# Moving the forget gate's chain from the pa projection into the v projection, and the norm's token-half sums to pa's second block

## The chip, the cores and the metric

The kernel runs on one core of one Trainium2 chip. The metric is the device time of one execution in microseconds, the median of several runs. Five engines work side by side, each in the order of its own instruction queue: TensorE (PE, matmuls), VectorE (DVE), ScalarE (ACT), GpSimd (POOL) and SyncE (SP), which here only issues DMAs. SBUF is the on-chip working memory, PSUM holds matmul results in eight banks.

## The reference

One layer of a hybrid encoder on x of 512 tokens by 1024 channels, in float32. What the change touches is the first part:

```python
h = rms_norm(x, mix_norm_pre[layer])
proj = jnp.einsum("bsd,de->bse", h, w_in[layer])
xa, ga, q, k, v, f_logit, g_a, g_b = jnp.split(proj, offs, axis=-1)
...
y_a = jax.nn.gelu(ga) * hr
y_b = forgetting_attention(q, k, v, f_logit + b_forget[layer])
merged = (jax.nn.sigmoid(g_a + b_merge[layer, 0]) * jnp.einsum("bse,ed->bsd", y_a, w_proj_a[layer])
          + jax.nn.sigmoid(g_b + b_merge[layer, 1]) * jnp.einsum("bse,ed->bsd", y_b, w_proj_b[layer]))
...
cum = jnp.cumsum(jax.nn.log_sigmoid(f_logit.astype(jnp.float32)), axis=1).transpose(0, 2, 1)
sc = sc + cum[:, :, qs:qe, None] - cum[:, :, None, :qe]
```

Here hr is the RG-LRU's scan over the convolved xa, 1280 channels wide. The forget gate is a projection of h onto 16 columns, one for each head, then log-sigmoid and a running sum over the tokens. Its result is needed as an additive bias when the attention scores are made, far behind the projections.

## The kernel before, in words

The normalised h is kept transposed in SBUF as two parts, hh (rounded to float32r) and hl (the rest), each 128 partitions by 8 by 512. A weight tile likewise becomes wh and wl: DMA into raw, ACT rounds it to wh (L198), DVE subtracts to get wl (L201). A product is three matmuls, wh·hh, wh·hl and wl·hh (mm3, L243).

The list `order` (L212) fixes the sequence of weight tiles: xa (10 tiles), v (8 units), ga (10), pa (16 units of 640 columns), q and k. `unit(name)` (L237) gives a tile and fetches two ahead; raw, wh and wl have four buffers each, so a tile's split waits for matmuls on the one four before it. `background` (L173) lets POOL make a small copy from a weight tile and issue one or two transfers for the last stage.

Outside blocks under `manual_schedule`, the framework's planner fixes every engine's order before the run: an instruction that comes earlier in the program goes first as soon as its inputs are there by the planner's own estimates. On the chip each engine then keeps that order and waits on semaphores. Pools with `reuse_waits="tile"` hand over memory tile by tile: a new tile waits for the last users of the tiles that lay there before. Pools on side "right" are stacked from the other end of SBUF.

The stages around the change, in the order of the program:

- Line 741: xa, with the RG-LRU's convolution (pool xc), its gate matmuls (`gate_mm`, three tiles behind, pool rgw), and at the end the first half of v, with the last gates between its units.
- Line 804: `v_out(0)` empties v's first four banks; then the second half of v in four units (L806), with tanh and exp of the RG-LRU on ACT (`batch`, in an order held together by `last_act`) and `inflow` on DVE.
- Line 816: ga, ten tiles; beside them sqrt, the scans (DVE, L789 and L790) and `gate_out` (gelu on ACT, product and split on DVE), which gives yh and yl. Pools rtanh (ten tiles tt) and gelu are on the right, in the scope rg2.
- Line 903: pa, y_a @ w_proj_a, in 16 steps of `PA_ORDER`: half 0 of columns 0 to 2, half 1 of columns 0 to 2, then alternating. Behind the matmuls of each step `early_sums(step)` is called.
- Line 956: q0 and k0, then the gates gA and gB by a seven-product scheme in a hand-written order, which needs sums of h's quarters.

Before the change, `early_sums(3)` called `forget()` (L832) and closed rg2. `forget` loads the 16 columns (L837), splits them into a 48-column tile fw (POOL memset L839, ACT L840, DVE L841), makes 16 matmuls (L844, L845), and runs a chain of small operations on 16 partitions by 512: ACT copy, bias add, log1p of exp by a series (L296 to L310, with one reciprocal and one Exp), a scan over the tokens (L856), and a reordering into keys (L858), which four DMAs on SP write to DRAM (L860). Its tiles came from rtanh's slots (tag "tt"). At step 3 the pools gkeep, gsum and hf were opened, in memory that rtanh and gelu had. The quarter sums of hh + hl, tiles hf (L883, L885 and two steps of `sub`, L351), were formed at steps 6 to 11, the first gate pair was loaded at 12 and its weight sums formed at 13.

Of the kernel before, what the change touches and what calls it, by code (L numbers as in the profile page):

```python
# [8 lines left out]
F32 = mybir.dt.float32  # L9
F32R = mybir.dt.float32r  # L10
BF16 = mybir.dt.bfloat16
AF = mybir.ActivationFunctionType
ALU = mybir.AluOpType
# [3 lines left out]
P = 128  # L17
S = 512
D = 1024
KD = D // P  # L20
NT = S // P
# [5 lines left out]
H = 16  # L27
# [8 lines left out]
C_CFW, C_CFB, C_MA, C_MB, C_BF = 80, 224, 272, 280, 288  # L36
# [17 lines left out]
PO = [0, 128, 384, 768, 1280]  # L54
# [7 lines left out]
def turns(ap, d=HT):  # L62

    if ap.shape[-1] == 2 * d:
        return ap.rearrange("p (a i) -> p i a", a=2)
    return ap.rearrange("p (t a i) -> p t i a", a=2, i=d)


def parted(ap, d=HT):

    if ap.shape[-1] == 2 * d:
        return ap.rearrange("p (i a) -> p a i", a=2)
    return ap.rearrange("p (t i a) -> p t a i", a=2, i=d)


def placed(ap, d=HT):

    if ap.shape[-1] == 2 * d:
        return ap.rearrange("p (a i) -> p a i", a=2)
    return ap.rearrange("p (t a i) -> p t a i", a=2, i=d)  # L80
# [7 lines left out]
def kernel(  # L88
# [15 lines left out]
    nc = tc.nc  # L104
    act, dve, pool, pe = nc.scalar, nc.vector, nc.gpsimd, nc.tensor
# [17 lines left out]
    def bank(name):  # L123
        return pspools[-1].tile([P, 512], F32, tag="ps", name=name)
# [12 lines left out]
    cpt = cpool.tile([P, NC], F32, name="cpt")  # L137
# [99 lines left out]
    def unit(name, ahead=2):  # L237

        i = where[name]
        fetch(i + ahead)  # L240
        return ready.pop(name)
# [54 lines left out]
    def log1p_exp_neg(z, tl):  # L296
        y = tl("y")
        dve.scalar_tensor_tensor(out=y, in0=z, scalar=-1.0, in1=z, op0=ALU.mult, op1=ALU.max)
        act.activation(out=y, in_=y, func=AF.Exp, scale=-1.0)
        d = tl("d")  # L300
        dve.tensor_scalar(out=d, in0=y, scalar1=2.0, scalar2=None, op0=ALU.add)
        dve.reciprocal(d, d)
        s = tl("s")
        dve.tensor_tensor(out=s, in0=y, in1=d, op=ALU.mult)
        dve.tensor_tensor(out=d, in0=s, in1=s, op=ALU.mult)
        dve.tensor_scalar(out=y, in0=d, scalar1=1.0 / 17.0, scalar2=None, op0=ALU.mult)
        for c in (15, 13, 11, 9, 7, 5, 3):
            dve.scalar_tensor_tensor(out=y, in0=y, scalar=1.0 / c, in1=d, op0=ALU.add, op1=ALU.mult)
        dve.scalar_tensor_tensor(out=s, in0=y, scalar=1.0, in1=s, op0=ALU.add, op1=ALU.mult)
        return s  # L310
# [5 lines left out]
    hh = hpool.tile([P, KD, S], F32R, name="hh")  # L316
    hl = hpool.tile([P, KD, S], F32R, name="hl")
# [6 lines left out]
    def v_start(c):  # L324
        for p in range(4 * c, 4 * c + 4):
            vt[p] = vpools[c].tile([P, NT, 4, HD], F32R, tag="vy", name=f"v{p}")
        return [bank(f"v{c}_{t}") for t in range(NT)]

    def v_mm(u, pv, w):
        wh, wl = w  # L330
        for t in range(NT):
            tok = slice(t * P, (t + 1) * P)
            for i in range(2):
                k = 2 * u + i
                pe.matmul(pv[t], hh[:, k, tok], turns(wh[:, i], SH), start=k == 0, stop=False)  # L335
                pe.matmul(pv[t], hh[:, k, tok], turns(wl[:, i], SH), start=False, stop=False)  # L336
                pe.matmul(pv[t], hl[:, k, tok], turns(wh[:, i], SH), start=False, stop=k == KD - 1)

    def v_out(c, pv):
        for t in range(NT):  # L340
            pvv = pv[t].rearrange("p (q j d) -> p q j d", q=4, j=2)
            for q in range(4):
                p = 4 * c + q
                vh = vt[p][:, t, 0:4:3, :]
                act.copy(vh, pvv[:, q])
                dve.tensor_tensor(out=vt[p][:, t, 1:3, :], in0=pvv[:, q], in1=vh.bitcast(F32), op=ALU.subtract)
# [3 lines left out]
    def sub(out, a, b):  # L350
        dve.tensor_tensor(out=out, in0=a, in1=b, op=ALU.subtract)  # L351
# [173 lines left out]
    with ExitStack() as rg:  # L525
        rt, ixt, tt = {}, {}, {}
# [267 lines left out]
        def gate_out(t):  # L794
# [6 lines left out]
            dve.tensor_tensor(out=placed(yl[t], SH), in0=parted(gl, SH), in1=placed(yh[t].bitcast(F32), SH),  # L801
                              op=ALU.subtract)

        v_out(0, pv)
        pv = v_start(1)
        for u in range(4):  # L806
            w = unit(f"v1_{u}")
            v_mm(u, pv, w)
            background(1, w)
            for t in range(5 * u // 2, 5 * (u + 1) // 2):  # L810
                batch([rg_tanh(t), rg_exp(t)])
                inflow(t)
        v_out(1, pv)
        steps = {0: (range(0, 4), ()), 1: (range(4, TR), range(0, 2)), 2: ((), range(2, 5)), 3: ((), range(5, 7)), 4: ((), range(7, 9)), 5: ((), range(9, TR))}
        outs = {2: (0,), 3: (1,), 4: (2, 3), 5: (4,), 6: (5,), 7: (6, 7), 8: (8,), 9: (9,)}
        for t in range(TR):
# [10 lines left out]

        papool = mstk.enter_context(tc.tile_pool(name="pa", bufs=1, reuse_waits="tile"))
        pa = papool.tile([P, KD, S], F32, name="pa")
        cnd = ctx.enter_context(tc.tile_pool(name="cnd", bufs=1, space=bass.MemoryType.DRAM)).tile([H, PO[NT]], F32, name="cnd")  # L830

        def forget():  # L832
            def tl(name, n=H, dt=F32):
                return tpool.tile([P, S], dt, tag="tt", name=f"f_{name}")[0:n]

            fr = tl("fr", P)[:, : KD * H].rearrange("p (k e) -> p k e", k=KD)
            nc.sync.dma_start(fr, w_f)  # L837
            fw = tl("fw", P, F32R)[:, : KD * 48].rearrange("p (k e) -> p k e", k=KD)
            pool.memset(fw[:, :, H:32].bitcast(F32), 0.0)  # L839
            act.copy(fw[:, :, 0:H], fr)  # L840
            dve.tensor_tensor(out=fw[:, :, 32:48], in0=fr, in1=fw[:, :, 0:H].bitcast(F32), op=ALU.subtract)  # L841
            pf = bank("f")
            for k in range(KD):
                pe.matmul(pf[0:48], fw[:, k], turns(hh[:, k]), start=k == 0, stop=False)  # L844
                pe.matmul(pf[0:48], fw[:, k], turns(hl[:, k]), start=False, stop=k == KD - 1)  # L845
            z = tl("z")
            act.copy(z, pf[32:48])
            dve.scalar_tensor_tensor(out=z, in0=pf[0:H], scalar=cpt[0:H, C_BF : C_BF + 1], in1=z, op0=ALU.add, op1=ALU.add)
            with tc.issue_after(last_act[0].ins):
                l1p = log1p_exp_neg(z, tl)  # L850
            dve.tensor_scalar(out=z, in0=z, scalar1=0.0, scalar2=None, op0=ALU.min)
            dve.scalar_tensor_tensor(out=z, in0=l1p, scalar=-2.0, in1=z, op0=ALU.mult, op1=ALU.add)
            ones = tl("ones")
            pool.memset(ones, 1.0)
            cum = tl("cum")
            dve.tensor_tensor_scan(out=cum, data0=ones, data1=z, initial=0.0, op0=ALU.mult, op1=ALU.add)  # L856
            keys = tl("keys")
            dve.tensor_scalar(out=placed(keys), in0=parted(cum), scalar1=-8.0, scalar2=None, op0=ALU.mult)  # L858
            for b in range(NT):
                nc.sync.dma_start(cnd[:, PO[b] : PO[b + 1]], keys[:, : PO[b + 1] - PO[b]])  # L860

        tgpool = mstk.enter_context(tc.tile_pool(name="tg", bufs=3, reuse_waits="tile"))
        gdram = ctx.enter_context(tc.tile_pool(name="gdram", bufs=1, space=bass.MemoryType.DRAM))
# [3 lines left out]
        gp = {}  # L867
# [2 lines left out]
        fq = []  # L870

        def early_sums(step):
            if step == 3:
                forget()
                rg2.close()
                gates.kpool = dstk.enter_context(tc.tile_pool(name="gkeep", bufs=2, reuse_waits="tile"))
                gates.tpool = sumstk.enter_context(tc.tile_pool(name="gsum", bufs=2, reuse_waits="tile"))
                hfpool = hfstk.enter_context(tc.tile_pool(name="hf", bufs=1, reuse_waits="tile"))
                fq.extend(hfpool.tile([P, KH, SH], F32, name=f"hf{i}") for i in range(4))
            elif 6 <= step < 10:  # L880
                i = step - 6
                k, c = (slice(0, KH), slice(KH, KD))[i % 2], (X, Y)[i // 2]
                dve.tensor_tensor(out=fq[i], in0=hh[:, k, c].bitcast(F32), in1=hl[:, k, c].bitcast(F32), op=ALU.add)  # L883
            elif step == 10:
                dve.tensor_tensor(out=fq[3], in0=fq[2], in1=fq[3], op=ALU.add)  # L885
                sub(fq[2], fq[0], fq[2])
            elif step == 11:
                sub(fq[0], fq[3], fq[0])
                sub(fq[1], fq[1], fq[0])
            elif step == 12:  # L890
                gp[0] = Pair(gates, 0, GP[0])
            elif step == 13:
                gp[0].sums(0)
                gp[0].sums(1)
            elif step == 14:
                gp[0].sums_hi(0)
                gp[0].sums_lo(0)
            elif step == 15:
                gp[0].sums_hi(1)
                gp[0].sums_lo(1)  # L900
# [896 lines left out]
```

## Time and profile before

| what | before |
|---|---|
| median of 3 runs | 887.05 us (886.27 to 887.78) |
| the profiled execution | 886.33 us, of it span 884.6 us |
| PE busy in the span | 871.0 us, 98% |
| DVE busy | 744.6 us, 84% |
| ACT busy | 611.1 us, 69% |
| v, second half on PE | 106.8 to 127.5 us |
| ga on PE | 127.5 to 179.3 us |
| pa with f's matmuls on PE | 179.3 to 234.6 us |
| granted PE clock in these stages | 1.00 |

A line of the timeline has the start in the span, the duration, the engine, the source line, the operation and the tiles as out<-in; a bracket at its end gives the engine's idle time before it and what ended that. A matmul's duration is modelled and overlaps the next one: a matmul of 512 columns starts 0.216 us after the one before it.

### The profile page before, as it was taken

What the parts mean: (1) busy time and instruction counts of PE and PEld (TensorE: products, weight loads), DVE (VectorE), ACT (ScalarE), POOL (GpSimd) and SP (SyncE); (2) the same over time, 40 slices, a digit from 0 to 9 for tenths busy, and PEclk for the clock granted to TensorE, in tenths of its full rate; (3) what the DMA queues carried; (4) which work ended last, traced back from release to release, by engine and by line L of the source; (5) the groups of instructions that cost most, each with busy time, mean ns of one, the idle gap of its engine ahead of it and who ended that gap; (6) DMA issues with size and microseconds to landing.
All of it is one profiled execution on the core that took longest, in us unless ns stands there. A gap on an engine that the chain in (4) does not pass through costs nothing.

```text
span 884.6 us, 15833 instructions
## 1 busy us (share of the span) xinstructions
PE 871.0 (98%) x5856; PEld 794.5 (90%) x5856; DVE 744.6 (84%) x1209; ACT 611.1 (69%) x1031; POOL 215.4 (24%) x278
## 2 busy tenths in 40 slices
PE   9999999999999999999999999999999999999996
PEld 7888888888899988888888889999999999988885
DVE  7986469738978849998868699999999999889997
ACT  6575595533466648776755497888888888688774
POOL 3344334536011013121104100233332332100000
PEclk9999999999999999999999999999999999999999
DMA  7787689999874377353506663778898898699864
GB/s 268 231 273 220 172 228 258 238 277 197 192 182 135 116 261 274 132 171 129 202 26 202 218 200 107 175 183 236 217 222 244 211 226 208 223 399 307 276 192 149
DMA packets 71040, 185.24 MB, mean 209 GB/s; under 512 B 7153, under 2 KB 27681, under 8 KB 70578
## 3 DMA queue, kind: packets, MB, share of 16 engines
q1 hardware_dynamic: 47360, 127.72, 43.2%
q0 software_dynamic: 23456, 56.37, 29.3%
q8 instruction: 46, 0.75, 0.3%
q14 instruction: 32, 0.26, 0.1%
q10 hardware_dynamic: 146, 0.14, 0.0%
HBM read 150.69 MB, written 35.73 MB: 211 GB/s over the span
## 4 chain that ended last, share of the span: by engine, by line
PE 85%; DVE 9%; ACT 2%; issue 2%; DMA 1%; DVEq 0%; SPq 0%; ACTq 0%
PE up L458 7%; PE up L456 7%; PE up L455 7%; PE dn L1500 2%; PE dn L1499 2%; PE dn L1498 2%; PE ga L245 2%; PE ga L244 2%; PE ga L246 2%; DVE al L351 2%; PE pa L245 2%; PE pa L244 2%; PE v L335 2%; PE v L336 2%; PE xa L244 2%
## 5 line engine op out<-in xcount | busy, mean ns | idle before, releaser
L1370 DVE SCALAR_TENSOR_TENSOR u<-up,cpt,u 128x511 f32<-128x511 f32 x96 | 71.3, 745 | 3.5 <-ACT u L1364 1.8
L391 POOL DMA_DIRECT2D ml<-raw_up x42 | 36.2, 861 | 148.1 <-ACT ml L390 88.8
L1500 PE MATMUL dn<-wh_dn,al 128*128 128x512 f32 (+1 forms) x180 | 66.5, 369 | 1.2 <-DVE al L351 1.2
L1499 PE MATMUL dn<-wl_dn,ah 128*128 128x512 f32 (+1 forms) x180 | 66.2, 368 | 0.5 <-DVE wl_dn L201 0.4
L1498 PE MATMUL dn<-wh_dn,ah 128*128 128x512 f32 (+1 forms) x180 | 65.7, 365 | 0.0
L455 PE MATMUL up<-sh,th 128*128 128x256 f32 x252 | 59.5, 275 | 0.0
L456 PE MATMUL up<-sl,th 128*128 128x256 f32 x252 | 59.5, 275 | 0.0
L201 DVE TENSOR_TENSOR wl_dn<-raw_dn,wh_dn 128x1024 fp32r<-128x1024 f32 x42 | 51.1, 1217 | 5.0 <-ACT wh_dn L198 5.0
L351 DVE TENSOR_TENSOR tl<-t,th 128x1024 fp32r<-128x1024 f32 x42 | 51.1, 1218 | 0.0
L1364 ACT ACTIVATE u<-up,cpt 128x512 f32<-128x512 f32 x48 | 36.9, 778 | 19.9 <-PE up L458 10.0
L455 PEld LDWEIGHTS up<-sh,th 128*128 128x128 f32 x252 | 48.4, 192 | 0.0
L456 PEld LDWEIGHTS up<-sl,th 128*128 128x128 f32 x252 | 48.4, 192 | 0.0
L198 ACT CAST wh_dn<-raw_dn 128x1024 fp32r<-128x1024 f32 x42 | 44.3, 1054 | 4.7 <-DMA raw_dn<-td 2.8
L437 ACT CAST th<-t 128x1024 fp32r<-128x1024 f32 x42 | 43.8, 1045 | 2.6 <-DVE t L351 0.6
L1378 POOL TENSOR_TENSOR yf<-u,u 128x512 f32<-128x512 f32 x23 | 30.4, 1323 | 58.8 <-issue 46.0
L1500 PEld LDWEIGHTS dn<-wh_dn,al 128*128 128x128 f32 x180 | 34.1, 189 | 7.5 <-DVE al L351 3.5
L456 PE MATMUL up<-h2l,mh 128*128 128x256 f32 x168 | 39.7, 275 | 0.0
L455 PE MATMUL up<-h2h,mh 128*128 128x256 f32 x168 | 39.7, 275 | 0.0
L1499 PEld LDWEIGHTS dn<-wl_dn,ah 128*128 128x128 f32 x180 | 34.1, 189 | 6.0 <-DVE wl_dn L201 1.8
L1054 ACT ACTIVATE P<-P,mx 128x384 f32<-128x384 f32 (+3 forms) x64 | 35.2, 552 | 5.1 <-DVE mx L1049 5.1
L458 PE MATMUL up<-sh,tl 128*128 128x256 f32 x252 | 38.4, 275 | 0.0
L1498 PEld LDWEIGHTS dn<-wh_dn,ah 128*128 128x128 f32 x180 | 34.1, 189 | 4.0
(729 smaller groups left out, 3230.2 us busy)
## 6 DMA issues: line engine op xcount, KB each, us to landing
raw_up<-in_w_up_dram SPq DMA_DIRECT2D x48, 512.0 KB, 5.3
td<-in_w_down_dram POOLq DMA_DIRECT2D x36, 512.0 KB, 7.1
raw_dn<-td SPq DMA_DIRECT2D x24, 512.0 KB, 4.9
ml<-raw_up POOLq DMA_DIRECT2D x21, 512.0 KB, 5.3
B<-cnd POOLq DMA_DIRECT2D x16, 640.0 KB, 5.4
raw_dn<-in_w_down_dram SPq DMA_DIRECT2D x18, 512.0 KB, 4.2
raw_wo<-in_w_out_dram SPq DMA_DIRECT2D x16, 512.0 KB, 4.2
td<-td POOLq DMA_DIRECT2D x12, 512.0 KB, 12.5
```

The costliest lines, as they stand in the source:

```text
L198: act.copy(self.wh, self.raw)
L201: engine.tensor_tensor(out=self.wl, in0=self.raw, in1=self.wh.bitcast(F32), op=ALU.subtract)
L244: pe.matmul(dst, ah, bh, start=first, stop=False)
L351: dve.tensor_tensor(out=out, in0=a, in1=b, op=ALU.subtract)
L437: act.copy(self.th[i], self.t[i])
L455: pe.matmul(dst, wh[:, k], turns(ah[:, k]), start=first and k == 0, stop=False, skip_group_check=True)
L456: pe.matmul(dst, wh[:, k], turns(al[:, k]), start=False, stop=False, skip_group_check=True)
L458: pe.matmul(dst, wl[:, k], turns(ah[:, k]), start=False, stop=k == KH - 1, skip_group_check=True)
L1370: dve.scalar_tensor_tensor(out=c[:, s:], in0=ps[:, : S - s], scalar=col(C_CFW + 3 * e + j), in1=c[:, s:], op0=ALU.mult, op1=ALU.add)
L1498: pe.matmul(d[:, x], ah[:, k, tok], bh, start=first, stop=False, skip_group_check=True)
L1499: pe.matmul(d[:, x], ah[:, k, tok], bl, start=False, stop=False, skip_group_check=True)
L1500: pe.matmul(d[:, x], al[:, k, tok], bh, start=False, stop=last, skip_group_check=True)
```

## The change

`forget()` becomes a generator with two stops: the first part loads and splits the weights, makes the matmuls and takes the tile z; the second adds the bias and runs the log1p series; the third does the rest and writes the keys. It is advanced at the head of the last v units 0, 1 and 2, ahead of that unit's matmuls in the program. Its tiles come from a pool of their own, "forget", one buffer for each of nine names (2 KB a partition each), opened on the right side when v's second half starts and closed behind `v_out(1)`.

In pa, rg2 is closed and the three pools are opened at step 0; the quarter sums stand at steps 1 to 6 (before 6 to 11), the first gate pair's load at step 11 (before 12) and its weight sums at step 12 (before 13). The splits at 14 and 15 stay.

```diff
+        cnd = ctx.enter_context(tc.tile_pool(name="cnd", bufs=1, space=bass.MemoryType.DRAM)).tile([H, PO[NT]], F32, name="cnd")
+        def forget():
+            def tl(name, n=H, dt=F32):
+                return fpool.tile([P, S], dt, name=f"f_{name}")[0:n]
...
+            for k in range(KD):
+                pe.matmul(pf[0:48], fw[:, k], turns(hh[:, k]), start=k == 0, stop=False)
+                pe.matmul(pf[0:48], fw[:, k], turns(hl[:, k]), start=False, stop=k == KD - 1)
+            z = tl("z")
+            yield
+            act.copy(z, pf[32:48])
+            dve.scalar_tensor_tensor(out=z, in0=pf[0:H], scalar=cpt[0:H, C_BF : C_BF + 1], in1=z, op0=ALU.add, op1=ALU.add)
+            with tc.issue_after(last_act[0].ins):
+                l1p = log1p_exp_neg(z, tl)
+            yield
+            dve.tensor_scalar(out=z, in0=z, scalar1=0.0, scalar2=None, op0=ALU.min)
...
         v_out(0, pv)
         pv = v_start(1)
+        fstk0 = rg2.enter_context(ExitStack())
+        fpool = fstk0.enter_context(tc.tile_pool(name="forget", bufs=1, side="right", reuse_waits="tile"))
+        fg = forget()
         for u in range(4):
             w = unit(f"v1_{u}")
+            next(fg, None)
             v_mm(u, pv, w)
...
         v_out(1, pv)
+        fstk0.close()
...
-        def forget():
-            def tl(name, n=H, dt=F32):
-                return tpool.tile([P, S], dt, tag="tt", name=f"f_{name}")[0:n]
...
         def early_sums(step):
-            if step == 3:
-                forget()
+            if step == 0:
                 rg2.close()
...
-            elif 6 <= step < 10:
-                i = step - 6
+            elif step < 5:
+                i = step - 1
...
-            elif step == 10:
+            elif step == 5:
...
-            elif step == 11:
+            elif step == 6:
                 sub(fq[0], fq[3], fq[0])
                 sub(fq[1], fq[1], fq[0])
+            elif step == 11:
+                gp[0] = Pair(gates, 0, GP[0])
             elif step == 12:
-                gp[0] = Pair(gates, 0, GP[0])
-            elif step == 13:
                 gp[0].sums(0)
                 gp[0].sums(1)
```

More of the change, by code (lines that the diff above doesn't have):

```diff
@@ L802, in gate_out @@
                               op=ALU.subtract)
+        cnd = ctx.enter_context(tc.tile_pool(name="cnd", bufs=1, space=bass.MemoryType.DRAM)).tile([H, PO[NT]], F32, name="cnd")
+        def forget():
+            def tl(name, n=H, dt=F32):
+                return fpool.tile([P, S], dt, name=f"f_{name}")[0:n]
+            fr = tl("fr", P)[:, : KD * H].rearrange("p (k e) -> p k e", k=KD)
+            nc.sync.dma_start(fr, w_f)
+            fw = tl("fw", P, F32R)[:, : KD * 48].rearrange("p (k e) -> p k e", k=KD)
+            pool.memset(fw[:, :, H:32].bitcast(F32), 0.0)
+            act.copy(fw[:, :, 0:H], fr)
+            dve.tensor_tensor(out=fw[:, :, 32:48], in0=fr, in1=fw[:, :, 0:H].bitcast(F32), op=ALU.subtract)
+            pf = bank("f")
+            for k in range(KD):
[9 more added lines that the diff above has]
+            dve.tensor_scalar(out=z, in0=z, scalar1=0.0, scalar2=None, op0=ALU.min)
+            dve.scalar_tensor_tensor(out=z, in0=l1p, scalar=-2.0, in1=z, op0=ALU.mult, op1=ALU.add)
+            ones = tl("ones")
+            pool.memset(ones, 1.0)
+            cum = tl("cum")
+            dve.tensor_tensor_scan(out=cum, data0=ones, data1=z, initial=0.0, op0=ALU.mult, op1=ALU.add)
+            keys = tl("keys")
+            dve.tensor_scalar(out=placed(keys), in0=parted(cum), scalar1=-8.0, scalar2=None, op0=ALU.mult)
+            for b in range(NT):
+                nc.sync.dma_start(cnd[:, PO[b] : PO[b + 1]], keys[:, : PO[b + 1] - PO[b]])
         v_out(0, pv)
         pv = v_start(1)
+        fstk0 = rg2.enter_context(ExitStack())
+        fpool = fstk0.enter_context(tc.tile_pool(name="forget", bufs=1, side="right", reuse_waits="tile"))
+        fg = forget()
         for u in range(4):
             w = unit(f"v1_{u}")
+            next(fg, None)
             v_mm(u, pv, w)
@@ L829 @@
         pa = papool.tile([P, KD, S], F32, name="pa")
-        cnd = ctx.enter_context(tc.tile_pool(name="cnd", bufs=1, space=bass.MemoryType.DRAM)).tile([H, PO[NT]], F32, name="cnd")
-        def forget():
-            def tl(name, n=H, dt=F32):
-                return tpool.tile([P, S], dt, tag="tt", name=f"f_{name}")[0:n]
[L836 to L860, printed above, removed]
         tgpool = mstk.enter_context(tc.tile_pool(name="tg", bufs=3, reuse_waits="tile"))
```

## The prediction

> **What bounds the kernel now.** I read the page first, then the waits of PE, then the windows by stage.
>
> ```profile
> span 884.6 us, 15833 instructions
> PE 871.0 (98%) x5856; PEld 794.5 (90%) x5856; DVE 744.6 (84%) x1209; ACT 611.1 (69%) x1031; POOL 215.4 (24%) x278
> ...
> 102.00:127.30 25.30, 25.30 (x118) 22.15 (x118) 15.47 (x30) 23.89 (x45) 10.98 (x13) 1.00 0.65 180
> 127.30:179.10 51.80, 51.80 (x241) 45.36 (x240) 43.52 (x64) 30.36 (x55) 21.74 (x29) 1.00 1.05 262
> 196.00:235.00 39.00, 39.00 (x182) 33.98 (x180) 32.48 (x40) 13.27 (x19) 15.55 (x16) 1.00 1.02 213
> 235.00:260.00 25.00, 23.84 (x167) 22.24 (x167) 20.07 (x24) 17.49 (x25) 2.62 (x3) 1.00 0.59 147
> ```
>
> A window's columns are its bounds and length, then the busy time of PE, PEld, DVE, ACT and POOL, the granted clock, the DMA share and GB/s. PE is busy for 98% of the span, and in the last v block, in ga and in pa it has no idle time at all: 25.30 of 25.30, 51.80 of 51.80, 39.00 of 39.00. Moving work between those stages cannot shorten them unless it takes matmuls out, and this change takes none out. Only the window behind pa, 235 to 260 us, has a hole: 25.00 − 23.84 = 1.16 us. The timeline of PE and its waits name it:
>
> ```profile
> 234.59 0.38 PE L244 MATMUL q<-hh,wh_q 128*128 128x512 f32 x1
> 236.11 0.48 PE L246 MATMUL q<-hh,wl_q 128*128 128x512 f32 x1 [0.93 <-DVE wl_q L201]
> 250.55 0.38 PE L455 MATMUL ma<-gsh,gth 128*128 128x256 f32 x1 [0.23 <-DVE ma L474]
> ```
>
> Two waits, 0.93 + 0.23 = 1.16 us, both on DVE. The chain that ended last agrees; it leaves PE for DVE here and nowhere before within pa:
>
> ```profile
> 224.88 2.35 DVE hf L883 x2
> ...
> 234.92 1.13 DVE wl_q L201
> ...
> 248.72 1.05 ACT gth L437
> ```
>
> Why DVE is late is in its own timeline, with the queues of ACT and SP beside it:
>
> ```profile
> 219.20 0.83 DVE L201 TENSOR_TENSOR wl_pa<-raw_pa,wh_pa 128x640 fp32r<-128x640 f32 x1 [1.99 <-ACT wh_pa L198]
> 222.61 4.63 DVE L883 TENSOR_TENSOR hf<-hh,hl 128x1024 f32<-128x1024 f32 x4 [2.58 <-DMA cnd<-f_keys]
> 227.89 1.22 DVE L885 TENSOR_TENSOR hf<-hf,hf 128x1024 f32<-128x1024 f32 x1
> 233.10 1.22 DVE L351 TENSOR_TENSOR hf<-hf,hf 128x1024 f32<-128x1024 f32 x1
> 234.84 1.22 DVE L201 TENSOR_TENSOR wl_q<-raw_q,wh_q 128x1024 fp32r<-128x1024 f32 x1
> 226.52 1.06 ACT L198 CAST wh_q<-raw_q 128x1024 fp32r<-128x1024 f32 x1 [0.88 <-DMA raw_q<-in_w_in_dram]
> 216.50 1.73 SPq L860 DMA_DIRECT2D cnd<-f_keys x4
> ```
>
> The hf tiles lie in memory that the forget chain still held, so the sums could start only when the keys had left for DRAM (issued 216.50, waited for until 222.61). Eight sums, 4.63 us for the first four and 1.22 us each for four more (9.5 us), then stand in front of wl_q. Its input wh_q was done at 226.52 + 1.06 = 227.58; wl_q started 7.3 us later, at 234.84.
>
> **The change, part by part.** *The sums, from pa's second block on.* With the forget chain in a pool of its own, hf waits only for the last tt tile, which the scans have finished long before pa. The 9.5 us of sums go into pa's first half. What they find there is the forget chain's empty place:
>
> ```profile
> 196.50:216.50 20.00, 20.00 (x95) 17.50 (x94) 18.55 (x25) 8.23 (x13) 12.17 (x12) 1.00 0.93 191
> L201 DVE TENSOR_TENSOR wl_pa<-raw_pa,wh_pa 128x640 fp32r<-128x640 f32 x6 | 4.8, 800 | 0.7 <-ACT wh_pa L198 0.7
> L302 DVE RECIPROCAL f_d<-f_d 16x512 f32<-16x512 f32 x1 | 3.3, 3340 | 0.0
> ```
>
> DVE was busy for 18.55 of these 20.00 us, 4.8 of it with wl_pa, so the chain took 18.55 − 4.8 = 13.8 us, more than the 9.5 that come in. Then wl_q can run from 227.6 and be done by 228.8. PE needs it for q's third matmul, at 235.0 without the wait, so over 6 us are to spare and the 0.93 us go. Everything on DVE and ACT behind wl_q (wl_k, gsl, gml, gt, gth) moves up with it, since ACT's copies of pa and gsh no longer queue behind a late gth. The add of the first gate pair, which cost 0.23 us because its input on ACT came behind gth (248.72 + 1.05), then goes as well. What is late next is gml for the first gate product; it has the same DVE chain in front of it and moves up more than PE does. Term: −0.93 − 0.23 = **−1.16 us**. Gp[0]'s load moves one step up as well; it changes no PE wait.
>
> *The matmuls of f.* Sixteen of them leave pa and enter the last v block.
>
> ```profile
> 192.28 0.38 PE L844 MATMUL f<-hh,f_fw 128*48 128x512 f32 x1
> 195.74 0.38 PE L244 MATMUL pa<-yh,wh_pa 128*128 128x512 f32 x1
> 91.89 0.38 PE L584 MATMUL gate<-halo_h,gh 96*128 96x512 f32 x1
> 99.68 0.38 PE L246 MATMUL gate<-halo_h,gl 112*128 112x512 f32 x1
> 106.59 0.38 PE L584 MATMUL gate<-halo_h,gh 96*128 96x512 f32 x1
> 106.81 0.38 PE L335 MATMUL v<-wh_v,hh 128*128 128x512 f32 x1
> L840 ACT CAST f_fw<-f_fr x1: 289/289/289, 138.9 to 138.9; 128x128 fp32r<-128x128 f32 x1
> L841 DVE TENSOR_TENSOR f_fw<-f_fr,f_fw x1: 291/291/291, 158.4 to 158.4; 128x128 fp32r<-128x128 f32 x1
> DMA to landing us min/median/max: 5.0/5.0/5.0
> ```
>
> They take 195.74 − 192.28 = 3.46 us of PE in either place: 0. In the program they stand right behind the last recurrent gate's matmuls, so on PE at about 106.8. Before, they had their weights 34 us early (158.4 against 192.3); now they need them there. The small load needs 5.0 us to land, then 0.29 us on ACT and 0.29 on DVE. The first two tiles of the new pool (load and split weights) lie, by the sizes of the pools on both sides, over the conv tiles xl of channel tiles 7 and 8, whose last readers are the gate matmuls that end at 92.1 and 99.9 (the gates 7 and 8; the third pair, to 106.81, is gate 9). So the load can be issued in the nineties and the weights stand by 102 or so. I take 0, in a range from 0 (no gain is possible where PE is never idle) to the whole path behind 106.81, 5.0 + 0.29 + 0.29 = 5.6 us, if the load must wait for the last gate.
>
> The profile's end shows what a longer hole does to the clock:
>
> ```profile
> 876.89 0.28 PE L1500 MATMUL dn<-wh_dn,al 128*128 128x256 f32 x1
> 880.00:882.00 2.00, 0.00 (x0) 0.00 (x0) 1.37 (x3) 0.00 (x0) 0.00 (x0) 0.94 0.64 246
> 882.00:884.60 2.60, 0.00 (x0) 0.00 (x0) 0.00 (x0) 0.00 (x0) 0.00 (x0) 0.50 0.34 118
> ```
>
> PE's last matmul ended at 877.2 and the granted clock fell to 0.50 just before 882, after some 4.6 us of nothing; a hole of 5.6 us could do the same. The Trainium skill, "TensorE: Matmul & The Clock Gate", section "What's actually happening", gives the rule: the array's clock is halved after at least one idle window of about 3.4 us, and is full again after at least one busy window of that length. By that rule the 5.6 us would cost an estimated 1.7 us more (3.4 us at half speed); the trace agrees with it as far as its end goes, and the forecast, which has no such hole, stays as it is.
>
> *The forget chain on DVE.* 13.8 us (more like 15 if it finds nothing to interleave with) move into the stretch where DVE feeds ga:
>
> ```profile
> 110.30:129.20 18.90, 18.90 (x89) 16.56 (x88) 12.01 (x20) 18.68 (x31) 8.04 (x9) 1.00 0.81 196
> 129.20:157.90 28.70, 28.70 (x135) 25.13 (x134) 28.65 (x44) 16.86 (x34) 11.40 (x16) 1.00 1.08 293
> 156.72 1.20 DVE L201 TENSOR_TENSOR wl_ga<-raw_ga,wh_ga 128x1024 fp32r<-128x1024 f32 x1
> 164.23 0.38 PE L246 MATMUL ga<-hh,wl_ga 128*128 128x512 f32 x1
> ```
>
> DVE has 18.90 − 12.01 = 6.9 us free up to 129.2 and none up to 157.9, so 13.8 to 15.5 − 6.9 = 6.9 to 8.6 us of delay lie on DVE through half of ga. The unit with the least cover is the eighth: its low part is done at 157.9 and read at 164.23, which the moved matmuls put off to 167.7, so 9.8 us are covered. It fits, with 1 to 3 us left: 0. If that cover fails, each us beyond it is one us of PE. No part of this can gain either: PE is never idle in that stretch.
>
> *SP, ACT, POOL.* SP issues the keys' four DMAs (1.73 us) among ga's loads and not before pa's last; it may sit waiting for the keys, which is the same cover as above. ACT saves a table load beside the forget Exp and pays it at the first gate tanh; POOL's two memsets feed only this chain. 0 each.
>
> Sum on the profiled execution: 886.33 us (span 884.6 and 1.7 around it) − 1.16 = 885.2. That execution lies 0.72 below the median of the runs, so on that scale 887.05 − 1.16 = **885.9 us**, or −0.13%. A measurement of this kernel can tell about 0.2%, 1.8 us, from no change: faster means below 885.3, slower above 888.8.
>
> **Rivals.** *More comes back than the profiled run shows.* The median is 0.72 us above it; if that is more of the same two DVE waits, −1.16 − 0.72 = −1.9 gives 885.2. For it: a wait on the end of a long DVE and DMA chain (raw_pa, keys) is what varies from run to run. Against it: PE has other waits, at the start and the end.
>
> *Nothing comes back.* The 9.5 us of sums stay late (the planner fits them in behind the wl_pa units), or the 0.93 us reappear as a wait for wl_k or in the first gate pair. That gives 887.05, or 886.8 if the 0.23 us alone go. Against it is the 7.3 us by which wl_q's input was early.
>
> *Slower: f's matmuls wait in the v block.* The place is PE at 106.8, where nothing can overtake the first f matmul; the price is up to 5.6 − 1.16 = +4.4 us, 891.5, and about +1 (888) if the planner puts part of v's first unit in front. It decides from where the load lands later than about 106. Against it: the layout above. The delay of ga's low parts beyond their 9.8 us would be seen in the other stage and is counted with the forecast's spread.
>
> **Numbers.** Forecast 0.57, of which a fifth falls below 885.3 by the spread of the runs (887.78 − 886.27 = 1.5 us); more gain 0.13; nothing 0.16; slower rival 0.14, nearly all above 888.8 or close to it. Faster: 0.57 / 5 + 0.12 = 0.23. Slower: 0.13. Same: 0.64. Range 884.8 to 888.8: below, the larger gain less a quarter of the spread; above, the rival at its small price; its full price is left out.
>
> **What would show it.** Right: no wait of PE for wl_q, hf done on DVE before pa's last third, f's matmuls at about 107 without idle time before them, the window behind pa 1.1 us fuller, ga's matmuls dense. Wrong: an idle time on PE ahead of f's first matmul or of a ga matmul on wl_ga, wl_q still behind hf, or a new wait of PE between 230 and 260 that sums to a us.

## The result and the profile after

The changed kernel took 893.25 us in the median of four runs (893.11 to 893.45), the kernel before beside it 886.87 (886.27 to 887.78): a ratio of 1.0074 with a 95% interval of 1.0062 to 1.0086. It is 6.4 us slower, where 885.9 was forecast. The profiled execution took 893.11 us, of it span 891.3; before it was 886.33 and 884.6.

The list of PE's waits in the changed kernel (total, times, longest) has a new first line; q's wait for wl_q, which was in the old list, is gone.

```profile
PE f L818 <- DVE f_fw L815: 6.7, 1, 6.7
PE xa L623 <- DVE ones L626: 1.5, 1, 1.5
```

The timeline of the changed kernel, rows of PE, SP, ACT and DVE around that wait:

```profile
105.68 0.38 PE L584 MATMUL gate<-halo_h,gh 96*128 96x512 f32 x1
112.75 0.63 PE L818 MATMUL f<-hh,f_fw 128*48 128x512 f32 x1 [6.69 <-DVE f_fw L815]
113.18 0.63 PE L819 MATMUL f<-hl,f_fw 128*48 128x512 f32 x1
118.94 0.38 PE L335 MATMUL v<-wh_v,hh 128*128 128x512 f32 x1
...
106.98 0.33 SPq L192 DMA_DIRECT2D raw_ga<-in_w_in_dram  x1
107.36 0.42 SPq L811 DMA_DIRECT2D f_fr<-in_w_f_dram  x1
...
111.99 0.30 ACT L814 CAST f_fw<-f_fr 128x128 fp32r<-128x128 f32 x1 [0.46 <-DMA f_fr<-in_w_f_dram]
112.32 0.29 DVE L815 TENSOR_TENSOR f_fw<-f_fr,f_fw 128x128 fp32r<-128x128 f32 x1
...
105.73 1.23 DVE L201 TENSOR_TENSOR wl_v<-raw_v,wh_v 128x1024 fp32r<-128x1024 f32 x1 [0.62 <-ACT wh_v L198]
```

Read it backwards. f's first matmul waits for the split weights (112.32 + 0.29 = 112.61). They wait for the load, issued only at 107.36, 1.5 us after PE had run out of gate matmuls. On SP it stands right behind a load of ga's weights (106.98), and that one waits for its raw buffer, which the split of a v unit frees (105.73 + 1.23 = 106.96). The load itself waits for nothing more: the one semaphore in its record last moved at 93.39. The answer of the trace on SP's waits says the same:

```profile
SPq L192 <- DVE wl_v L201: 3.2, 1, 3.2
```

The wait is not all. The windows of the changed kernel (bounds, length, busy PE, PEld, DVE, ACT and POOL, granted clock, DMA share, GB/s):

```profile
102.00:105.90 3.90, 3.90 (x19) 3.22 (x17) 2.62 (x11) 3.10 (x11) 0.07 (x1) 1.00 0.08 35
105.90:112.75 6.85, 0.16 (x1) 0.03 (x1) 3.71 (x8) 6.33 (x13) 3.44 (x5) 0.66 0.48 163
112.75:118.94 6.19, 6.19 (x16) 3.08 (x17) 2.77 (x4) 6.03 (x10) 0.00 (x0) 0.55 0.00 0
...
243.20:268.70 25.50, 25.50 (x186) 24.18 (x185) 18.61 (x24) 17.81 (x26) 2.62 (x3) 1.00 0.72 164
```

f's sixteen matmuls took 118.94 − 112.75 = 6.19 us at a mean clock of 0.55; at full clock they took 3.46 before. The matmul at 113.18 starts 0.43 us after the one before it, twice the 0.216 of full speed. The last row answers to 235 to 260 of before: behind pa, PE now has no hole.

So the loss is in one place. By the starts on PE, after against before (the differences are of the unrounded starts):

| on PE | before | after | difference |
|---|---|---|---|
| last gate matmul | 106.59 | 105.68 | −0.91 |
| ga's first matmul | 127.53 | 139.66 | +12.13 |
| q's first matmul | 234.59 | 243.26 | +8.68 |
| k's first matmul | 240.96 | 248.44 | +7.48 |
| gate products, first | 246.14 | 253.62 | +7.48 |
| attention's first pt | 343.24 | 349.68 | +6.44 |
| last matmul | 876.89 | 883.67 | +6.79 |

The −0.91 comes out of the start (that matmul lies anywhere from 105.6 to 107.7 in the kernels whose program is nearly the same up to it). From there to ga 13.04 us are added: f's 3.46, which left pa (12.13 − 8.68 = 3.45), 6.85 of hole and 2.73 of half clock. From q to pt 8.68 − 6.44 = 2.24 us come back. −0.91 + 6.85 + 2.73 − 2.24 = +6.43 at pt, and 0.35 more by the end; the span grew by 6.7.

### The profile page after: what moved, and what is told of

Read it like the earlier page. It is cut to its first block, busy times and chain, and to the rows that moved or that the text cites. A ratio compares the mean times of both kernels' runs of the same rounds, so it can differ in the third digit from the quotient of the medians.

```text
span 891.3 us, 15838 instructions
## 1 busy us (share of the span) xinstructions
PE 872.9 (98%) x5856; PEld 794.8 (89%) x5856; DVE 743.7 (83%) x1209; ACT 612.1 (69%) x1031; POOL 214.3 (24%) x278
## 4 chain that ended last, share of the span: by engine, by line
PE 89%; DVE 6%; ACT 2%; issue 2%; DMA 1%; DVEq 0%; ACTq 0%; SPq 0%
PE up L458 7%; PE up L456 7%; PE up L455 7%; PE dn L1507 3%; PE dn L1506 2%; PE dn L1505 2%; PE pa L244 2%; PE ga L245 2%; PE ga L244 2%; PE pa L246 2%; PE pa L245 2%; PE ga L246 2%; PE q L244 2%; PE xa L244 2%; PE q L246 2%; PE q L245 2%
```

## The experiments

Theory: the sums' new steps and the forget chain's leaving pa give their gain, and the whole loss is f's load that comes too late, with the clock behind it. Rivals: the sums' new steps or the moved DVE chain carry part of the loss. The kernel before ran beside each group, at 886.97 to 887.43 us.

**e1, the load early.** f's two weight tiles get a pool of their own, opened before the xa loop; load and split are put ahead of v's first half. Everything else is as changed.

```diff
+            rg2 = rg.enter_context(ExitStack())
+            fwpool = rg2.enter_context(tc.tile_pool(name="forgetw", bufs=1, side="right", reuse_waits="tile"))
             for t in range(NF, TR + NF):
+                if t == TR:
+                    fr = fwpool.tile([P, S], F32, name="f_fr")[:, : KD * H].rearrange("p (k e) -> p k e", k=KD)
+                    nc.sync.dma_start(fr, w_f)
...
+                    act.copy(fw[:, :, 0:H], fr)
+                    dve.tensor_tensor(out=fw[:, :, 32:48], in0=fr, in1=fw[:, :, 0:H].bitcast(F32), op=ALU.subtract)
```

> The changed kernel, with the load and the split of the forget weights issued ahead of v's first half (a pool of two tiles beside the gates' pool); the matmuls stay where the change put them. Theory (PE waits 6.7 us for the weights, then runs some 5.5 us at half clock, 2.7 us lost): f's matmuls start at once behind the last gate, no drop of the clock, 893.25 - 9.5 = 883.8 us, under the kernel before by about 3. Rival (the moved chain itself costs, on DVE and ACT beside ga): the wait goes but PE stalls on wl_ga or yl in ga instead, and the time stays above 888.

884.24 us, ratio 0.9972 (0.9962 to 0.9982). With memory that nobody holds, the planner put the load far ahead; a view of the load's tile, then the timeline of PE in e1:

```profile
L746 SPq DMA_DIRECT2D f_fr<-in_w_f_dram x1: 426/426/426, 24.8 to 24.8; - x1
```

```profile
106.08 0.38 PE L584 MATMUL gate<-halo_h,gh 96*128 96x512 f32 x1
106.30 0.38 PE L820 MATMUL f<-hh,f_fw 128*48 128x512 f32 x1
106.52 0.38 PE L821 MATMUL f<-hl,f_fw 128*48 128x512 f32 x1
```

The matmuls stand where the prediction put them, without a gap, and 9.0 us of 893.25 are gone: 6.85 + 2.73 = 9.58 were to go. The theory holds, and the change without its hole is a gain of 0.3%. The edit moved the load's memory and its place in the program together, so it does not tell which of the two the planner went by.

**e2, PE kept busy in the hole.** Thirty matmuls, whose result is overwritten, stand ahead of f's; they add work and leave nothing out.

```diff
+            for i in range(30):
+                pe.matmul(pf, hh[:, i % KD, 0:P], hh[:, i % KD], start=True, stop=True)
             for k in range(KD):
```

> The changed kernel with 30 matmuls of 512 columns ahead of f's own, into the same bank, where they are overwritten; PE is busy (30 x 0.216 = 6.5 us) while the weights are on their way. Theory: the end of the weights' load sets the start of f's matmuls as before (112.8), but the clock stays at 1.00 and f takes 3.5 us instead of 6.2: 893.25 - 2.7 = 890.5 us. Rival (the clock falls for the 48-column matmuls, which load the array little, and not for the hole): the clock still falls and the time stays at 893.2.

892.98 us, ratio 1.0069 (1.0056 to 1.0083): only 0.3 us under the changed kernel, not 2.7. The clock did what was expected, by the windows of e2:

```profile
105.90:113.20 7.30, 7.30 (x33) 5.83 (x31) 3.88 (x8) 6.74 (x14) 3.55 (x5) 1.00 0.46 153
113.20:116.70 3.50, 3.50 (x17) 2.08 (x17) 1.39 (x2) 3.40 (x6) 0.00 (x0) 1.00 0.02 5
```

f's matmuls ran at full clock in 3.5 us. But the profiled execution, at 899.79 the longest of the six, has a wait that no kernel had before:

```profile
PE k L244 <- ACT wh_k L198: 3.5, 1, 3.5
```

It appeared 130 us behind the edit; e3 shows where such a wait comes from, and the longest tick of ga took 18.21 us here. Whether the other five runs lost their gain in a smaller wait of that kind, no profile shows.

**e3, f's matmuls one v unit later.** One more stop of the generator, between split and matmuls.

```diff
             dve.tensor_tensor(out=fw[:, :, 32:48], in0=fr, in1=fw[:, :, 0:H].bitcast(F32), op=ALU.subtract)
+            yield
             pf = bank("f")
```

> The changed kernel with one more stop in the forget chain, between the split of the weights and the matmuls, so that the matmuls and all behind them stand one unit of v (5.2 us) later in the program. Theory: of the wait of 6.7 us some 1.5 us are left or none, no drop of the clock, 884 to 885.5 us. Rival (DVE beside ga is the bound): the keys come 5 us later, ga's low parts run out of cover and the time stays above 888.

896.72 us, ratio 1.0114 (1.01 to 1.0127): a miss of 11 us. The hole at f was gone (0.7 us left), and the wait of e2 had grown instead. PE's waits of e3, and its timeline:

```profile
PE k L244 <- ACT wh_k L198: 7.7, 1, 7.7
...
PE f L819 <- DVE f_fw L815: 0.7, 1, 0.7
```

```profile
247.76 1.04 ACT L198 CAST wh_k<-raw_k 128x1024 fp32r<-128x1024 f32 x1 [5.44 <-POOL tick L175]
...
143.64 28.94 POOL L175 COPY tick<-wh_ga 128x1 f32<-128x1 f32 x1 [1.84 <-ACT wh_ga L198]
172.51 2.04 POOL L156 DMA_DIRECT2D td<-td  x2
...
246.52 1.01 POOL L156 DMA_DIRECT2D td<-td  x1 [5.28 <-DMA td<-td]
247.15 0.58 POOL L175 COPY tick<-wh_pa 128x1 f32<-128x1 f32 x1
```

ACT can't cast k0's weights before POOL has read the tile that had the buffer. That read is a tick, the copy of one column (`background`, L175) that paces the last stage's transfers td. The ticks were late because one of them, in ga, had taken 28.94 us for 128 elements.

**e4, the sums at their old steps.** In the changed kernel the sums, the first pair and the closing of rg2 go back to steps 3 and 6 to 13.

```diff
-            if step == 0:
+            if step == 3:
...
-            elif step < 5:
-                i = step - 1
+            elif 6 <= step < 10:
+                i = step - 6
```

> The changed kernel with the sums, the first gate pair's load and its sums back at the old steps (3, 6 to 11, 12 and 13); only the forget move is left. Theory (the sums are early because their memory and DVE are free, whatever their step): 893.2 us, wl_q still early. Rival (the step sets it): the 0.9 us at wl_q come back, 894.2 us or more.

893.37 us, ratio 1.0074 (1.0061 to 1.0086): as the changed kernel. The sums' steps are not the loss. They did not make the sums early either: DVE formed them from 168.5 to 185.2 us here and from 168.0 to 184.7 in the changed kernel, both in ga, and at 222.6 to 234.3 before. From q to k, PE had 5.18 us here too, as in the changed kernel, and 6.37 before. That the times are equal is luck in part, by the profiled executions. f's matmuls took 4.84 us here against 6.19, since the half clock ended 2.79 us behind their start and not 5.53; a new wait of PE took as much back:

```profile
PE ma L455 <- DVE ma L474: 1.5, 1, 1.5
```

The chain before it goes back to a tick again: one in ga took 12.32 us, and ACT's cast of k0 waited 4.2 us for POOL.

**e5, e6 and e7, attempts on the ticks that failed.** To free e3 of the tick, e5 leaves it out and asks that the transfers be issued behind ACT's cast of the unit; e6 keeps the copy but lets it read a constant column; e7 is e1 with e5's edit.

```diff
-        i = pool.tensor_copy(out=tick, in_=w[0].bitcast(F32)[:, 0, 0:1])
+        i = cur[0] or pool.tensor_copy(out=tick, in_=w[0].bitcast(F32)[:, 0, 0:1])
         with tc.issue_after(i.ins):
```

> The kernel of e3 (f's matmuls one v unit later), and GpSimd's one-column tick copies left out: each background transfer is issued behind ScalarE's cast of the same unit. In e3 the tick of the sixth ga unit took 28.94 us (143.64 to 172.51) while VectorE ran instructions with two inputs without a gap from 143.50 to 172.5, the transfers then ran late to 246.52, and k0's cast waited for the last tick. Theory (the tick is shut out by VectorE's two-input instructions): no such hole in GpSimd, last transfer by 235, no k wait, no half clock at q and k, 884 to 885.5 us, as e3 was meant to give. Rival (the transfers themselves were slow): last transfer still near 246, but k0 no longer tied to it, 884 to 886. Rival (k0's weights are late for another reason): k wait of 7 us stays, 896.

> The kernel of e3 with the tick kept, but reading one column of constants instead of the unit's high half, behind ScalarE's cast of that unit. The copy still reads, so it can still be shut out by VectorE; the slot of the high half is no longer tied to it. Theory: GpSimd again stands some 15 to 30 us in one tick in the ga stage, the last transfer is issued after 240, and k0 still does not wait: 884 to 886 us. Rival (late transfers themselves cost time, by what they do beside q and k): 890 or more with the k wait gone. Rival (k0 late for another reason): 896.

> The kernel of e1 (f's weights loaded and split before v) without ticks. In e1 the last transfer was issued at 233.94 and k0's cast was 4 us ahead of its need, so the ticks were off the path there. Theory: 883.5 to 884.5 us, no change from e1's 884.24, the last transfer earlier by some us. If the ticks or the slot's tie also cost time elsewhere (v, ga, pa): down to 882.

926.86 us (ratio 1.0451, 1.0435 to 1.0467), 931.26 (1.0503, 1.0488 to 1.0519) and 909.38 (1.0248, 1.023 to 1.0266), so far above every theory that the edit had done something else. `issue_after` orders the plan; across engines it left no wait in the built program. Nothing paced the transfers, and they crowded into the xa and gate stages, where before PE had no hole. Rows of e5's waits of PE and of its timeline:

```profile
PE f L821 <- POOL f_fw L815: 18.6, 1, 18.6
PE gate L586 <- DVE xc L542: 5.8, 1, 5.8
PE gate L246 <- DMA halo_h<-xh: 4.6, 2, 3.6
```

```profile
146.90 1.01 POOL L156 DMA_DIRECT2D td<-td  x1 [5.64 <-DMA td<-td]
```

The last transfer, at 228.32 before, was issued at 146.90, and f's memset stood behind them on POOL. Ticks are needed; these three say nothing on what delays them. That k0 did not wait in any of them fits the theory, but with everything else shifted it is no evidence.

**e9 and e10, the read alone.** ACT copies one column behind each cast into a tile of eight columns (0.19 us each). In e9 POOL overwrites that column with a constant, in e10 it copies the column onto itself. Both wait for the cast, neither ties the weight buffer to POOL; e10 reads, e9 does not. Both stand on e3.

```diff
             w.hi()
+            if n[:2] in ("xa", "ga", "pa") or n[:2] == "v1":
+                c = emitted[0] % 8
+                sc_of[n] = tick[:, c : c + 1]
+                act.copy(sc_of[n], w.wh[:, 0:1].bitcast(F32))
...
-        i = pool.tensor_copy(out=tick, in_=w[0].bitcast(F32)[:, 0, 0:1])
+            i = pool.memset(cur[0], 0.0)
```

In e10 the last line is `pool.tensor_copy(out=cur[0], in_=cur[0])`.

> The kernel of e3 with the tick changed: ScalarE copies one column behind each cast into a small tile, and GpSimd overwrites that column with a constant, so the tick still waits for the cast but reads nothing, and the high half's slot is not tied to GpSimd. This replaces the kernels without ticks, in which nothing paced the transfers any more. Theory (VectorE's two-input instructions shut out the reading tick): no tick over 5 us in the ga stage, the last transfer issued by 236, no k wait, no half clock at q and k: 884 to 886 us against e3's 896.7. Rival (the transfers themselves are slow to land): last transfer near 246 again, no k wait, 884 to 886. Rival (k0 late for another reason): k wait of 7 us, 896.

> As e9, but GpSimd copies that column onto itself, so the tick reads; the high half's slot is not tied to GpSimd here either. The only difference from e9 is the read. Theory (shut out by VectorE): again a tick of 15 to 30 us in the ga stage and a last transfer after 240, but no k wait, since the slot is free: 884 to 887 us. Rival (it is not the read): ticks and last transfer as in e9.

e9 took 884.63 us, ratio 0.9969 (0.9954 to 0.9984): 12 us less than e3 by the ticks alone, with f 0.5 us late and no wait of PE for k. e10 took 903.18, ratio 1.018 (1.0165 to 1.0196). The same tick of the same ga unit in the timelines of e9 and then e10:

```profile
144.91 0.10 POOL L178 MEMSET tick<- 128x1 f32 x1 [2.32 <-ACT tick L239]
145.15 2.04 POOL L156 DMA_DIRECT2D td<-td  x2
```

```profile
144.98 37.60 POOL L178 COPY tick<-tick 128x1 f32<-128x1 f32 x1 [2.26 <-ACT tick L239]
182.52 2.04 POOL L156 DMA_DIRECT2D td<-td  x2
...
260.60 2.19 POOL L400 DMA_DIRECT2D gml<-raw_ma  x2
```

0.10 against 37.60 us, and the transfers behind it go out at 145.15 against 182.52. The tick that reads is the one that is held up. DVE's windows in e9 show what POOL lived beside:

```profile
145.00:160.00 15.00, 15.00 (x71) 13.15 (x70) 15.00 (x18) 4.49 (x7) 3.25 (x7) 1.00 1.16 288
160.00:180.00 20.00, 20.00 (x94) 17.50 (x94) 20.00 (x25) 8.83 (x15) 5.94 (x11) 1.00 0.92 220
```

DVE has no pause there (15.00 of 15.00, 20.00 of 20.00), with subtractions, products and scans that take two tensors from SBUF. This is what the Trainium skill states in "SBUF — State Buffer", section "Who interferes with whom": a DVE instruction with two SBUF inputs contends with a GpSimd instruction that reads SBUF, not with one that only writes it. The two kernels agree with it, as far as one pair can.

e10's time missed its expectation by 16 us all the same. k0 was free, as expected, but the late transfers (the last at 259.85) now stood on POOL ahead of gml's load (260.60), and the gate products waited, by PE's waits of e10:

```profile
PE ma L467 <- DMA gml<-raw_ma: 14.0, 1, 14.0
```

The lateness was not removed, only handed to the next one in POOL's queue.

**e8, e11 and e12, the parts put together.** e8 is e1 with e4's old steps, e11 is e1 with e9's tick, e12 the changed kernel with e9's tick.

> The kernel of e1 with the sums at their old steps of pa (close at 3, sums 6 to 11, pair at 12 and 13). The step move was worth nothing beside the hole (e4 893.37 against 893.25). Theory (the gain of 2.2 us from q to pt is the forget gate's leaving pa, not the sums' steps): 884.2, at most 0.4 off. Rival (the steps carry a part of it once the hole is gone): 885 to 886, with a wait of ma for VectorE of 1 us or more, as e4 showed 1.5 us.

> The kernel of e1 (f's weights loaded and split before v) with the tick of e9. In e1 nothing waited for the ticks, so theory: 883.5 to 885 us, within 0.1% of e1's 884.24; the last transfer at 233.94 in e1 comes some us earlier, and k0's cast with it. More than 1 us under e1 would mean that the ticks cost time in v, ga or pa too.

> The changed kernel with the tick of e9 and nothing else: f's matmuls stay in front of v's second half, its weights' load stays behind the third ga load. Theory (two separate costs, and the changed kernel pays only the first): f waits 6 to 7 us for the split again, the clock halves behind it, 892.5 to 894 us, within 0.1% of 893.25. Rival (the ticks carry part of the changed kernel's loss): 888 to 891, with the f wait shorter or less behind it.

e8: 884.77 us, ratio 0.9975 (0.9966 to 0.9985). e11: 884.26, ratio 0.9965 (0.9952 to 0.9978). e12: 892.99, ratio 1.0063 (1.0046 to 1.0079). e11 and e12 came as the theory had them, e8 0.2 us above its bound. Without the hole the sums' steps are worth nothing that can be measured here (e8 against e1); with it, e4 cannot say, because the clock and the wait for ma differ too. Where f is on time and k0 covered, the tick costs nothing. And the changed kernel's loss is not in its ticks: with them mended f still waits.

```profile
PE f L827 <- DVE f_fw L824: 6.5, 1, 6.5
```

The kernels that beat both are e1, e8, e9 and e11, at 884.2 to 884.8 us; their intervals overlap.

## Why the prediction was wrong, point by point

**f's matmuls: the step that failed.** It said that "the load can be issued in the nineties and the weights stand by 102 or so. I take 0". On the chip the load waited for no memory: its record shows no wait for PE. Two other things were left out. One is SP's order: the planner put the load behind three ga loads, and the third could not go before 106.98, because its buffer hung on a split of v's weights. In the program the load stands ahead of these three, so by the planner's rule its inputs must have come later in the planner's own estimates. Whether that was the memory, and so whether the layout was read rightly, no run tried by itself. The other follows from it: a small load in a queue has the release of the instruction ahead of it as its own. The step had asked when the tile is free, and not what stands in front on SP. The prediction went over SP's order for the keys' DMAs, which cost nothing, and not for this load, which made the hole.

**The price of the late load.** The slower rival named this mechanism, its place and its deciding point (a landing later than about 106; it landed at some 111.9), with 0.14. Its bound was 5.6 us of hole; measured were 6.85, since the load left 1.5 us after the hole began, and took 4.5 us to land, not 5.0. Its upper price, 891.5, left the clock out. The sentence on the clock gate gave an estimated 1.7 us; 2.73 were measured in the changed kernel. In e12, with a hole of much the same length, f's sixteen matmuls took 4.80 us, 1.34 too many. The records of the granted clock say why. In the changed kernel it was halved from 108.04 to 118.28, and f started at 112.75, so 5.53 us of work ran at half clock; in e12 it was halved from 110.48 to 117.31, and f started at 114.59, which leaves 2.72. The rule agreed in kind only: in the changed kernel the clock fell 1.98 us after the last gate matmul's end (105.68 + 0.38 = 106.06), and in e12 it was back after those 2.72 us of work, both sooner than the window of about 3.4 us that the rule asks for. One window's worth was no upper bound.

**The gain behind pa: right, and too small.** −1.16 us were forecast from two waits; 2.24 came back between q and pt. PE's waits of before had more of that kind than the two that were counted:

```profile
PE q L246 <- DVE wl_q L201: 0.9, 1, 0.9
...
PE mb L455 <- DVE mb L474: 0.3, 1, 0.3
PE s2c L1040 <- DVE l_k L1024: 0.2, 1, 0.2
PE ma L455 <- DVE ma L474: 0.2, 1, 0.2
PE k L244 <- DVE mx L1049: 0.2, 1, 0.2
```

None of the five is in the changed kernel's list. A wait also costs more than its bracket: between q and k the start moved by 6.37 − 5.18 = 1.19 us for a wait of 0.93, because a matmul's duration in the profile overlaps its successor (0.38 us for one that starts the next 0.216 later), and the idle time is counted from its end. The cause was given to the wrong half of the edit: with the sums at their old steps, wl_q is on time in e4 and e8, and from q to pt e8 needs 106.68 us, e1 106.50 and the kernel before 108.65. What freed wl_q was the forget chain's leaving pa, not the new steps. The sums went further than the prediction had them, too: not into pa's first half, but into ga.

**The forget chain on DVE: right for PE, blind for POOL.** ga kept its cover: PE was idle neither in ga nor in pa, as forecast. "POOL's two memsets feed only this chain" was true and not enough. The chain and the sums together filled DVE in ga: 49.90 of 51.80 us of that stage, where it was 43.52 of 51.80 before. One of POOL's ticks in ga became long. The views of the tick tile in before, after and e3 (min, median and longest in ns, first and last start):

```profile
L175 POOL COPY tick<-wh_ga x10: 183/1170/2345, 114.1 to 164.2; 128x1 f32<-128x1 f32 x10
```

```profile
L175 POOL COPY tick<-wh_ga x10: 184/836/6979, 127.2 to 180.0; 128x1 f32<-128x1 f32 x10
```

```profile
L175 POOL COPY tick<-wh_ga x10: 185/1111/28936, 114.2 to 179.2; 128x1 f32<-128x1 f32 x10
```

In the changed kernel it cost nothing (e12), because q came 8.7 us later and so did the need for k0's weights. In e3, where the hole was closed, it took back more than the closing gave.

**SP, ACT.** The keys' DMAs (143.52 in the changed kernel, 1.73 us) cost nothing, as forecast.

What stays open: why a tick is shut out for 29 us in e3 and for 5.93 at most in e1. A full DVE alone does not do it: nine of the ten ga ticks of the kernel before ended without any idle time of DVE beside them, none over 2.35 us. The long tick of e10, which ended at 144.98 + 37.60 = 182.58, got in at the first idle time that DVE had since its start, between these two sums:

```profile
181.33 1.20 DVE L902 TENSOR_TENSOR hf<-hf,hf 128x1024 f32<-128x1024 f32 x1
182.56 1.23 DVE L360 TENSOR_TENSOR hf<-hf,hf 128x1024 f32<-128x1024 f32 x1
```

What lets the short ones in without a pause was not tried.

Also open is why the planner put f's load behind ga's.

## What to carry to other kernels

When a step is moved, ask of its first load not when its memory is free but what stands ahead of it in its queue, and what that is waiting for. An engine without a pause on the path is the one place where a step moved in front of it must have its operands early; a hole that is long enough to halve the clock costs more than its length (6.85 us cost 9.58 here, the 0.7 us of e3 did not halve it). And look at GpSimd's reads when more work goes beside them on VectorE: here one copy of a column was held up for tens of microseconds, and the bill came a stage later.

## What the runs showed of the hardware

- A GpSimd copy of one column took up to 37.60 us beside a VectorE that was busy for 37.50 of the 37.50 us from 145.0 on, a memset of the same column 0.10 us at the same place (e10, e9). In the kernel before, copies beside an equally busy VectorE took at most 2.35 us.
- A hole of PE of 3.5 us was enough to halve the clock in e2, one of 1.5 us in e4 was not. The half clock lasted well into the work behind the hole. A window of e2 around k0:

```profile
249.00:256.20 7.20, 6.26 (x14) 4.55 (x15) 6.11 (x6) 6.47 (x8) 0.00 (x0) 0.53 0.74 148
```

- In the records of the granted clock the stretches at 0.50 inside the kernels lasted from 3.41 us to 30.72 (in e6, beside a hole of 30.2), all multiples of 3.41; in the changed kernel three of them, from 108.04 to 118.28. The stretch at full clock behind that, 768.00 us to 886.28, is a multiple too (225). So the same hole costs more or less by its place: 2.73 us in the changed kernel, 1.34 in e12. The Trainium skill, "TensorE: Matmul & The Clock Gate", section "What's actually happening", says that the window runs freely; these multiples agree.
